# RWKV time mixing: both crossbar transposes in one-token rows, without shift copies

## The chip, the core and the metric

The kernel runs on one core of a Trainium2 chip. The metric is the time on the device in microseconds (us), median of several runs. A profile of one execution gives the span and what each engine did in it: TensorE (PE; PEld is its weight load), VectorE (DVE), ScalarE (ACT), GpSimd (POOL), and SyncE (SP), which here only issues DMAs.

## What is computed

The input x has 16 batches of 2048 tokens of 256 columns in float32. Each token is mixed with the one before it (the first token of a batch with zero), once for a value and once for a receptance; both go through a 256x256 matrix; the receptance goes through a sigmoid and gates the value; the product goes through a third matrix. The key is computed in the reference too, but nothing uses it.

```
x_prev[:, 1:] = x[:, :-1]
xv = x * time_mix_v + x_prev * (1 - time_mix_v)
xr = x * time_mix_r + x_prev * (1 - time_mix_r)
v = xv @ value_weight
r = xr @ receptance_weight
out = (sigmoid(r) * v) @ output_weight
```

## The kernel before

**Units.** A unit is 512 tokens of a batch, four units make a batch, and there are 64 of them. The matrices contract over the columns, so x must stand transposed in SBUF, with columns on the partitions (`xt`). For each unit g of the main loop (L614) TensorE makes the receptance (`psum_r`) and the value (`psum_v`) with `project`, four matmuls of 512 columns each, and the output (`psum_o`) of the unit before with eight matmuls of 256 columns (`out_matmuls`). ACT makes the sigmoid (`s_sb`, L626) and copies the output to SBUF (L440). VectorE multiplies the gate and the value (`z_sb`, L676).

**Mixing.** The coefficient of x is folded into the weights, so that the mixed operand is c * x_prev + x. The product c * x_prev (the "scaling") is made one or two units ahead, for a pair of units at once in the later part: half of it by VectorE (L340) or, from unit 34 (`FREE`) on, for one of the two operands by ACT (L606); the other half by GpSimd (L350). VectorE then adds x (L362). GpSimd's scaling of a unit is made to wait for a given addition of VectorE ("one at a time").

**Three ways into `xt`.** Batches 0 to 9 are loaded to SBUF as bf16 by GpSimd's DMAs (which cast) and transposed on TensorE (L274), with an ACT copy out of PSUM (L291). Batches 10 to 15 (`STAGED`) are cast into a DRAM buffer (`x_both` or `x_natural`) by the same kind of load, and go from there to SBUF by two DMA transposes on SP (`by_dma`, L247), one for 10 to 12 and one for 13 to 15. `T_AT` puts them at units 27 and 39.

- Batches 13 to 15: the DRAM buffer has one row per partition of x, 384 rows of 4096 columns (16 tokens each). In the transposed tile a token's predecessor stands in the slot before it, except for the first slot of each partition, which is filled by a shifted copy on ACT (`shift`, L639, two copies of 127 columns per batch, at the second unit of the batch before) and a memset on GpSimd (L220).
- Batches 10 to 12 (`NATURAL`): the DRAM buffer has one token a row, 256 columns, with 16 zero rows (`PAD`) ahead of each batch, written by six small DMAs on SP (L138): 6192 rows. In the transposed tile the predecessor is simply the column before, so `tokens` reads at an offset of one column and no shift is needed. The output of such a unit reads `z_sb` with a stride of four tokens (`natural=True`), and is stored in pieces of four rows of `out`.

**What keeps DMAs in order.** All stores but one are issued by SP, in program order; a pair of units is one store of 1 MB, named here by its odd unit (pair 25 is units 24 and 25). Each SP DMA waits for the eighth SP DMA before it, since eight semaphores are used in turn. [...] the first transpose waits for the whole of load 12, the loads of 13 to 15 (`STAGE_AT`, L685, issued by GpSimd at units 34, 35 and 36, behind its scaling in that unit) wait for the first transpose, and the second transpose waits for load 15. Loads 12 and 15 come as two halves (`HALVED`). `FIRST` names the pairs whose store is put off until just ahead of a transpose and waits for the first half of that load: pair 25 ahead of the first transpose, pair 29 ahead of the second. `WAITING` names the pairs whose store is put off until behind the second transpose: 31, 33 and 35. `dpool` has two DRAM buffers; output tiles come from `opool` (seven buffers) or, from pair 37 on, partly from `xpool`.

Of the kernel before, what the change touches and what calls it, by code (L numbers as in the profile page):

```python
# [9 lines left out]
BF16 = mybir.dt.bfloat16  # L10
# [5 lines left out]
def kernel(  # L16
# [37 lines left out]
    LONG = 8  # L54
    H = UJ // 2
    STAGED = 10
    BYDMA = NU - STAGED * UB
    CROSS = NU - BYDMA - LOOK
    FREE = CROSS
    LATE_O = CROSS - 2  # L60
    T_AT = {27: 10, 39: 13}
    FIRST = {25: 27, 29: 39}
    WAITING = {31: 39, 33: 39, 35: 39}
    STAGE_AT = {34: 13, 35: 14, 36: 15}
    GROUPS = [(2, 3), (4, 5, 6), (7, 8, 9), (10, 11, 12), (13, 14, 15)]
    HALVED = (12, 15)
    NATURAL = (10, 11, 12)
    PAD = 16
    SPARE = 9 * UB // 2
    NX, NO = 4, 7  # L70
# [19 lines left out]
    dpool = ctx.enter_context(tc.tile_pool(name="dpool", bufs=2, space=bass.MemoryType.DRAM))  # L90
    xtpool = ctx.enter_context(tc.tile_pool(name="xtpool", bufs=2))
# [15 lines left out]
    x_bf = {}  # L107
    x_both = {}
    loads = {}
    xt_both = {}  # L110
    xt = {}
# [17 lines left out]

    def new_staged(b, group):  # L130

        if b not in NATURAL:
            x_both[b] = dpool.tile([len(group), P, J, D], BF16, name="x_both")
            return
        x_both[b] = dpool.tile([len(group), PAD + S, D], BF16, name="x_natural")
        for h in range(KO):
            for k in range(len(group)):
                nc.sync.dma_start(  # L138
                    out=x_both[b][k, :PAD, h * P : (h + 1) * P], in_=zeros[k * PAD : (k + 1) * PAD]
                )  # L140

    def load(b):
        if b >= STAGED:
            group = next(q for q in GROUPS if b in q)
            if b == group[0]:
                new_staged(b, group)
            x_bf[b] = x_both[group[0]][b - group[0]]
            if b in NATURAL:
                x_bf[b] = x_bf[b][PAD:].rearrange("(p j) d -> p j d", p=P)
        else:  # L150
            x_bf[b] = xpool.tile([P, J, D], BF16, name="x_bf")
        if b < BYUNIT:
# [11 lines left out]
        return nc.gpsimd.dma_start(out=x_bf[b], in_=rows(b), max_dma_last_dim=run)  # L164
# [4 lines left out]
    for m, tm in enumerate([time_mix_r, time_mix_v]):  # L169
        nc.scalar.dma_start(  # L170
            out=tm_rows[m * KO : (m + 1) * KO, :], in_=tm.rearrange("(ko p) -> ko p", p=P)
        )

    def load_halves(e):
# [8 lines left out]
        out=w_f32[:, 0], in_=receptance_weight.rearrange("(ko p) n -> p ko n", p=P)  # L183
# [25 lines left out]
    def new_xt(b):  # L209
        if b >= BYUNIT:  # L210
            for group in GROUPS:
                if b != group[0]:
                    continue
                if b in NATURAL:
                    xt_both[b] = xtpool.tile([P, KO, len(group) * (PAD + S)], BF16, name="xt_both")
                    return
                xt_both[b] = xtpool.tile([P, J + 1, KO, len(group), P], BF16, name="xt_both")
                for k in range(len(group)):
                    xt[b + k] = xt_both[b][:, :, :, k]
                    nc.gpsimd.memset(xt[b + k][:, 0, :, 0:1], 0.0)  # L220
# [26 lines left out]
    def by_dma(b, after):  # L247

        new_xt(b)
        if b in NATURAL:  # L250
            op = nc.sync.dma_start_transpose(
                out=xt_both[b], in_=x_both[b].rearrange("b s d -> (b s) d")
            )
        else:
            op = nc.sync.dma_start_transpose(
                out=xt_both[b][:, 1:].rearrange("p j k b c -> p (j k) (b c)"),
                in_=x_both[b].rearrange("b p j d -> (b p) (j d)"),
            )
        tc.add_manual_dep(op.ins, after.ins.name, SYNC, reason="not beside a load")
        return op  # L260

# [54 lines left out]
    def slots(piece, off=0):  # L316

        b, _, lo, hi = piece
        j = lo // P + (lo // TU if b < BYUNIT else 0) + off
        return slice(j, j + (hi - lo) // P)  # L320

    def tokens(piece, off, ko=None):

        b, _, lo, hi = piece
        if b not in NATURAL:
            s = slots(piece, off)
            return xt[b][:, s] if ko is None else xt[b][:, s, ko]
        t = (b - NATURAL[0]) * (PAD + S) + PAD - 1 + off + lo
        cols = xt_both[NATURAL[0]][:, :, t : t + hi - lo].rearrange("p k (j c) -> p j k c", c=P)
        return cols if ko is None else cols[:, :, ko]  # L330

    def mixed(piece):
# [56 lines left out]
                stop=(n == len(parts) - 1),  # L389
            )  # L390

    def out_matmuls(ps, z, jj, slot, natural=False):
        by_slot = z.rearrange("p k (c j) -> p k j c" if natural else "p k (j c) -> p k j c", j=UJ)
        for ko in range(KO):
            nc.tensor.matmul(  # L395
                out=ps[:, slot, :],
                lhsT=by_slot[:, ko, jj],
                rhs=wo_bf[:, ko, :],
                start=(ko == 0),
                stop=(ko == KO - 1),  # L400
            )

    def store(queue, b, lo, hi, after=None):
        dst = out[b].rearrange("(p j) d -> p j d", p=P)
        src = o_sb[b, lo // (2 * UJ)]
        j = lo % (2 * UJ)
        op = queue.dma_start(out=dst[:, lo:hi, :], in_=src[:, j : j + hi - lo, :])
        if after is not None:
            tc.add_manual_dep(op.ins, after.ins.name, SYNC, reason="in turn with the last load")

    def out_part(pool, name, z, b, e, jj, n, copy, queue):
        ps = pool.tile([P, n, D], FP32, name=name)
        for k in range(n):
            out_matmuls(ps, z, jj + k, k)
# [12 lines left out]
    def output(g, z):  # L427
        b, e = divmod(g, UB)
        if e % 2 == 0:
            new_o(b, e // 2)  # L430
        o = o_sb[b, e // 2]
        j0 = e % 2 * UJ
        if g >= NU - 4:
            for h in range(2):
                out_part(ps_t_pool, "ps_t", z, b, e, h * H, H, nc.scalar.copy, nc.sync)
            return
        ps = ps_o_pool.tile([P, UJ, D], FP32, name="psum_o")
        for jj in range(UJ):
            out_matmuls(ps, z, jj, jj, b in NATURAL)
        nc.scalar.copy(out=o[:, j0 : j0 + UJ, :], in_=ps)  # L440
        if b < BYUNIT or b in NATURAL:
            if e % 2 == 1:
                nc.sync.dma_start(
                    out=unit_rows(out, b, e - 1, 2), in_=o.rearrange("p (e j) d -> p e j d", j=UJ)
                )
        elif g >= NU - 8:
            store(nc.sync, b, e * UJ, (e + 1) * UJ)
        elif e % 2 == 1:
            pair = (b, (e - 1) * UJ, (e + 1) * UJ)
            if g in FIRST:  # L450
                firsts.setdefault(FIRST[g], []).append(pair)
            elif g in WAITING:
                kept.setdefault(WAITING[g], []).append(pair)
            else:
                store(nc.sync, *pair)
# [158 lines left out]
    for g in range(NU - 1):  # L614
# [13 lines left out]
        if g in T_AT:  # L628
# [6 lines left out]
        by_crossbar = g // UB + 1 if g > CROSS and g % UB == 1 and g < NU - UB else None  # L635
        if by_crossbar in NATURAL:
            by_crossbar = None

        def shift(ko):  # L639
            if by_crossbar is not None:  # L640
                t = xt[by_crossbar]
                nc.scalar.copy(out=t[:, 0, ko, 1:P], in_=t[:, J, ko, 0 : P - 1])

        shift(1)
        if LATE_O < g < NU - 2:
            output(g - 2, z_prev2)
        shift(0)
        for p in products.get(g + 1, []):
            if g >= FREE and p[0][1] == 1:
                scale_act(p[0], (0,))  # L650
# [77 lines left out]
```

## Time and profile before

| what | us |
|---|---|
| median of 3 runs (lowest, highest) | 201.17 (200.4, 202.63) |
| the profiled execution | 201.63 |
| its span | 199.7 |
| PE busy | 191.9 |
| DVE busy | 185.0 |
| ACT busy | 178.2 |
| POOL busy | 83.9 |
| first transpose: issue, time to landing | 100.70, 17.7 |
| second transpose: issue, time to landing | 137.34, 17.3 |
| last matmul ends, last store issued | 194.3, 194.9 |

Times within a profile count from the start of the span. A line of the page's table of groups names the kernel's line, the engine, the operation and its operands; a timeline has start and duration in front, and in brackets how long the engine was idle before and whom it waited for. SPq is SP issuing DMAs; its duration is the issue, and the landing comes later. In the table by windows come, for PE, PEld, DVE, ACT and POOL, the busy time and the number of instructions, then the granted clock of TensorE, the mean share of the 16 DMA engines (over 1 when several packets are in flight in one engine) and the GB/s they moved.

### The profile page before, as it was taken

What the parts mean: (1) busy time and instruction counts of PE and PEld (TensorE: products, weight loads), DVE (VectorE), ACT (ScalarE), POOL (GpSimd) and SP (SyncE); (2) the same over time, 40 slices, a digit from 0 to 9 for tenths busy, and PEclk for the clock granted to TensorE, in tenths of its full rate; (3) what the DMA queues carried; (4) which work ended last, traced back from release to release, by engine and by line L of the source; (5) the groups of instructions that cost most, each with busy time, mean ns of one, the idle gap of its engine ahead of it and who ended that gap; (6) DMA issues with size and microseconds to landing.
All of it is one profiled execution on the core that took longest, in us unless ns stands there. A gap on an engine that the chain in (4) does not pass through costs nothing.

```text
span 199.7 us, 3815 instructions
## 1 busy us (share of the span) xinstructions
PE 191.9 (96%) x1389; PEld 123.7 (62%) x1389; DVE 185.0 (93%) x289; ACT 178.2 (89%) x203; POOL 83.9 (42%) x112
## 2 busy tenths in 40 slices
PE   8899999999999999999999998999999999999990
PEld 7456676666666666666666664666666665556660
DVE  1899999999999999999999999999999999999970
ACT  4699899999999999999999998999999999999970
POOL 1865543363542446332442437444444444444200
PEclk9999999999999999999999999999999999999998
DMA  5999999999999999999999999999999999999993
GB/s 174 229 189 216 216 281 273 277 283 274 291 313 292 217 265 279 322 288 315 334 406 251 207 359 200 215 197 275 209 241 346 440 405 403 408 404 431 396 382 133
DMA packets 37610, 58.10 MB, mean 291 GB/s; under 512 B 26068, under 2 KB 27352, under 8 KB 34520
## 3 DMA queue, kind: packets, MB, share of 16 engines
q1 hardware_dynamic: 33232, 41.34, 61.2%
q0 software_dynamic: 4208, 16.39, 41.5%
q8 instruction: 11, 0.18, 0.3%
q10 hardware_dynamic: 152, 0.13, 0.2%
q14 instruction: 7, 0.06, 0.1%
HBM read 34.34 MB, written 39.87 MB: 372 GB/s over the span
## 4 chain that ended last, share of the span: by engine, by line
PE 89%; DMA 4%; issue 1%; DVE 1%; ACT 1%; SPq 0%; POOL 0%; ACTq 0%
PE psum_v L370 27%; PE psum_r L370 26%; PE psum_o L395 26%; PE ps_t L274 8%; DMA x_bf<-in_x_dram 2%; DMA w_f<-n_receptance_weight_dram 2%; PE ps_t L395 1%; DVE z_sb L676 1%; ACT mix L606 1%; PE ps_t L370 0%; SPq L176 0%; POOL x_bf L194 0%; PE psum_r L395 0%; DVE x_bf L417 0%; PE psum_v L395 0%
## 5 line engine op out<-in xcount | busy, mean ns | idle before, releaser
L350 POOL TENSOR_SCALAR mix<-xt_both,c_sb 128x1024 bf16<-128x1024 bf16 (+1 forms) x55 | 61.2, 1113 | 87.7 <-DVE mix L362 87.7
L362 DVE TENSOR_TENSOR mix<-mix,xt_both 128x1024 bf16<-128x1024 bf16 x112 | 77.9, 705 | 1.4
L676 DVE TENSOR_TENSOR z_sb<-s_sb,psum_v 128x1024 bf16<-128x1024 bf16 (+1 forms) x64 | 76.7, 1200 | 2.4 <-PE psum_v L370 0.9
L370 PEld LDWEIGHTS <-w_bf 128*128 128x128 bf16 x516 | 48.9, 98 | 39.7 <-DVE mix L362 1.1
L626 ACT ACTIVATE s_sb<-psum_r 128x1024 bf16<-128x1024 f32 x63 | 65.2, 1036 | 6.0 <-PE psum_r L370 5.7
L370 PE MATMUL psum_v<-mix,w_bf 128*128 128x512 bf16 (+1 forms) x256 | 65.3, 377 | 0.3 <-DVE z_sb L676 0.2
L370 PE MATMUL psum_r<-mix,w_bf 128*128 128x512 bf16 (+1 forms) x252 | 64.2, 377 | 0.4 <-DVE mix L362 0.4
L395 PE MATMUL psum_o<-wo_bf,z_sb 128*128 128x256 bf16 x486 | 63.2, 273 | 0.0
L395 PEld LDWEIGHTS <-z_sb 128*128 128x128 bf16 x512 | 51.0, 101 | 18.7 <-DVE z_sb L479 0.8
L440 ACT COPY o_sb<-psum_o 128x1024 f32<-128x1024 f32 x50 | 51.2, 1024 | 4.9 <-PE psum_o L395 4.9
L291 ACT COPY xt_both<-ps_t 128x1024 bf16<-128x1024 bf16 x32 | 32.9, 1040 | 0.0
L274 PEld LDWEIGHTS <-x_bf 128*128 128x128 bf16 x304 | 19.6, 98 | 9.1 <-DMA x_bf<-in_x_dram 1.8
L274 PE MATMUL ps_t<-ident,x_bf 128*128 128x128 bf16 x304 | 22.7, 219 | 0.3 <-DMA x_bf<-in_x_dram 0.2
L340 DVE TENSOR_SCALAR mix<-xt_both,c_sb 128x1024 bf16<-128x1024 bf16 (+1 forms) x47 | 21.1, 458 | 0.0
L606 ACT ACTIVATE mix<-xt_both,c_sb 128x1024 bf16<-128x1024 bf16 x14 | 16.2, 1159 | 0.0
L362 DVE TENSOR_TENSOR mix<-mix,xt_first 128x1024 bf16<-128x1024 bf16 x15 | 10.6, 716 | 0.1
L440 ACT COPY x_bf<-psum_o 128x1024 f32<-128x1024 f32 x10 | 10.2, 1015 | 0.0
L340 DVE TENSOR_SCALAR mix<-xt_first,c_sb 128x512 bf16<-128x512 bf16 x22 | 6.5, 348 | 0.3 <-ACT xt_first L284 0.2
L291 ACT COPY xt_first<-ps_t 128x1024 bf16<-128x1024 bf16 x6 | 6.1, 1021 | 0.0
L164 POOL DMA_DIRECT2D x_bf<-in_x_dram x8 | 5.7, 714 | 0.0
L526 POOL COPY xt_first<-xt_first 128x254 bf16<-128x254 bf16 x5 | 2.0, 395 | 6.5 <-DVE mix L362 6.5
L350 POOL TENSOR_SCALAR mix<-xt_first,c_sb 128x512 bf16<-128x512 bf16 x6 | 4.1, 689 | 0.7 <-DVE mix L362 0.2
(72 smaller groups left out, 52.7 us busy)
## 6 DMA issues: line engine op xcount, KB each, us to landing
out_dram<-o_sb SPq DMA_DIRECT2D x24, 1024.0 KB, 15.9
x_bf<-in_x_dram POOLq DMA_DIRECT2D x8, 1024.0 KB, 19.1
out_dram<-x_bf SPq DMA_DIRECT2D x4, 1024.0 KB, 13.0
x_natural<-in_x_dram POOLq DMA_DIRECT2D x2, 1024.0 KB, 17.1
x_both<-in_x_dram POOLq DMA_DIRECT2D x2, 1024.0 KB, 9.4
x_bf<-in_x_dram POOLq DMA_DIRECT2D x6, 256.0 KB, 6.3
out_dram<-x_bf SPq DMA_DIRECT2D x6, 256.0 KB, 4.5
o_sb<-in_x_dram SPq DMA_DIRECT2D x4, 256.0 KB, 3.7
```

The costliest lines, as they stand in the source:

```text
L164: return nc.gpsimd.dma_start(out=x_bf[b], in_=rows(b), max_dma_last_dim=run)
L274: nc.tensor.transpose(out=ps[:, jj], in_=src[:, jj, ko * P : (ko + 1) * P], identity=idn)
L291: nc.scalar.copy(out=xt[b][:, j0 : j0 + UJ], in_=ps)
L340: nc.vector.tensor_scalar(out=mixed(piece)[:, :, ko], in0=tokens(piece, 0, ko), scalar1=c_sb[:, m, ko : ko + 1], scalar2=None, op0=ALU.mult,)
L350: op = nc.gpsimd.tensor_scalar(out=mixed(piece)[:, :, 1], in0=tokens(piece, 0, 1), scalar1=c_sb[:, m, 1:2], scalar2=1.0, op0=ALU.mult, op1 ...
L362: return nc.vector.tensor_tensor(out=mixed(piece), in0=mixed(piece), in1=tokens(piece, 1), op=ALU.add)
L370: nc.tensor.matmul(out=ps[:, mo, :], lhsT=w_bf[:, m, ko, mo * P : (mo + 1) * P], rhs=mixed((b, m, e * TU + lo, e * TU + hi))[:, :, ko], st ...
L395: nc.tensor.matmul(out=ps[:, slot, :], lhsT=by_slot[:, ko, jj], rhs=wo_bf[:, ko, :], start=(ko == 0), stop=(ko == KO - 1),)
L440: nc.scalar.copy(out=o[:, j0 : j0 + UJ, :], in_=ps)
L606: nc.scalar.activation(out=mixed(piece)[:, :, ko], in_=tokens(piece, 0, ko), func=ACT.Copy, scale=c_sb[:, m, ko : ko + 1],)
L626: nc.scalar.activation(out=s_sb, in_=ps_r, func=ACT.Sigmoid)
L676: nc.vector.tensor_tensor(out=z_sb[:, :, c : c + n], in0=s_sb[:, :, c : c + n], in1=ps_v[:, :, c : c + n], op=ALU.mult,)
```

## The change

Batches 13 to 15 are handled as 10 to 12 were. Both DRAM buffers have one token a row and are made at once, at the load of batch 10, so that twelve pad DMAs stand on SP where six stood. Both transposes have 6192 rows of 256 columns. `tokens` reads batches 10 to 15 at a column offset; the shift copies on ACT and the memsets for batches 13 to 15 go. The outputs of batches 13 to 15 are made with the stride over tokens and stored in pieces of four rows of `out` for a whole unit (of `n` rows for parts of a unit).

Three tables of the order change. The store of pair 23 is now the one just ahead of the first transpose, and that of pair 25 is put behind it. Pair 27 is the one just ahead of the second transpose, and pairs 29, 31, 33 and 35 stand behind it. Loads 13, 14 and 15 are issued at units 35, 36 and 37.

```diff
     T_AT = {27: 10, 39: 13}
-    FIRST = {25: 27, 29: 39}
-    WAITING = {31: 39, 33: 39, 35: 39}
-    STAGE_AT = {34: 13, 35: 14, 36: 15}
+    FIRST = {23: 27, 27: 39}
+    WAITING = {25: 27, 29: 39, 31: 39, 33: 39, 35: 39}
+    STAGE_AT = {35: 13, 36: 14, 37: 15}
-    NATURAL = (10, 11, 12)
...
     def new_staged(b, group):
-        if b not in NATURAL:
-            x_both[b] = dpool.tile([len(group), P, J, D], BF16, name="x_both")
-            return
         x_both[b] = dpool.tile([len(group), PAD + S, D], BF16, name="x_natural")
...
     def load(b):
         if b >= STAGED:
             group = next(q for q in GROUPS if b in q)
-            if b == group[0]:
-                new_staged(b, group)
-            x_bf[b] = x_both[group[0]][b - group[0]]
-            if b in NATURAL:
-                x_bf[b] = x_bf[b][PAD:].rearrange("(p j) d -> p j d", p=P)
+            if b == STAGED:
+                for q in GROUPS:
+                    if q[0] >= STAGED:
+                        new_staged(q[0], q)
+            x_bf[b] = x_both[group[0]][b - group[0], PAD:].rearrange("(p j) d -> p j d", p=P)
...
-                if b in NATURAL:
-                    xt_both[b] = xtpool.tile([P, KO, len(group) * (PAD + S)], BF16, name="xt_both")
+                if b >= STAGED:
+                    t = xtpool.tile([P, KO, len(group) * (PAD + S)], BF16, name="xt_both")
+                    for k in range(len(group)):
+                        xt[b + k] = t[:, :, k * (PAD + S) + PAD - 1 : (k + 1) * (PAD + S)]
+                    xt_both[b] = t
                     return
...
     def by_dma(b, after):
         new_xt(b)
-        if b in NATURAL:
-            op = nc.sync.dma_start_transpose(
-                out=xt_both[b], in_=x_both[b].rearrange("b s d -> (b s) d")
-            )
-        else:
-            op = nc.sync.dma_start_transpose(
-                out=xt_both[b][:, 1:].rearrange("p j k b c -> p (j k) (b c)"),
-                in_=x_both[b].rearrange("b p j d -> (b p) (j d)"),
-            )
+        op = nc.sync.dma_start_transpose(
+            out=xt_both[b], in_=x_both[b].rearrange("b s d -> (b s) d")
+        )
...
     def tokens(piece, off, ko=None):
         b, _, lo, hi = piece
-        if b not in NATURAL:
-            s = slots(piece, off)
-            return xt[b][:, s] if ko is None else xt[b][:, s, ko]
-        t = (b - NATURAL[0]) * (PAD + S) + PAD - 1 + off + lo
-        cols = xt_both[NATURAL[0]][:, :, t : t + hi - lo].rearrange("p k (j c) -> p j k c", c=P)
+        if b < STAGED:
+            cols = xt[b][:, slots(piece, off)]
+        else:
+            cols = xt[b][:, :, off + lo : off + hi].rearrange("p k (j c) -> p j k c", c=P)
         return cols if ko is None else cols[:, :, ko]
...
-    def out_matmuls(ps, z, jj, slot, natural=False):
-        by_slot = z.rearrange("p k (c j) -> p k j c" if natural else "p k (j c) -> p k j c", j=UJ)
-        for ko in range(KO):
+    def out_matmuls(ps, z, b, jj, n):
+        cols = z[:, :, jj * P : (jj + n) * P]
+        order = "p k (j c) -> p k j c" if b < STAGED else "p k (c j) -> p k j c"
+        slot = cols.rearrange(order, j=n)
+        for j in range(n):
+            for ko in range(KO):
...
     def store(queue, b, lo, hi, after=None):
-        dst = out[b].rearrange("(p j) d -> p j d", p=P)
         src = o_sb[b, lo // (2 * UJ)]
         j = lo % (2 * UJ)
-        op = queue.dma_start(out=dst[:, lo:hi, :], in_=src[:, j : j + hi - lo, :])
+        src = src[:, j : j + hi - lo, :]
+        if b < STAGED:
+            dst = out[b].rearrange("(p j) d -> p j d", p=P)[:, lo:hi, :]
+        else:
+            n = min(hi - lo, UJ)
+            dst = out[b, lo * P : hi * P].rearrange("(e p j) d -> p e j d", p=P, j=n)
+            src = src.rearrange("p (e j) d -> p e j d", j=n)
+        op = queue.dma_start(out=dst, in_=src)
...
-        def shift(ko):
-            if by_crossbar is not None:
-                t = xt[by_crossbar]
-                nc.scalar.copy(out=t[:, 0, ko, 1:P], in_=t[:, J, ko, 0 : P - 1])
-
-        shift(1)
         if LATE_O < g < NU - 2:
             output(g - 2, z_prev2)
-        shift(0)
```

More of the change, by code (lines that the diff above doesn't have):

```diff
@@ L390, in project_unmixed @@
             )
-    def out_matmuls(ps, z, jj, slot, natural=False):
-        by_slot = z.rearrange("p k (c j) -> p k j c" if natural else "p k (j c) -> p k j c", j=UJ)
-        for ko in range(KO):
[L395 to L401, printed above, removed]
+    def out_matmuls(ps, z, b, jj, n):
[4 more added lines that the diff above has]
+            for ko in range(KO):
+                nc.tensor.matmul(
+                    out=ps[:, j, :],
+                    lhsT=slot[:, ko, j],
+                    rhs=wo_bf[:, ko, :],
+                    start=(ko == 0),
+                    stop=(ko == KO - 1),
+                )
     def store(queue, b, lo, hi, after=None):
-        dst = out[b].rearrange("(p j) d -> p j d", p=P)
         src = o_sb[b, lo // (2 * UJ)]
         j = lo % (2 * UJ)
-        op = queue.dma_start(out=dst[:, lo:hi, :], in_=src[:, j : j + hi - lo, :])
+        src = src[:, j : j + hi - lo, :]
[6 more added lines that the diff above has]
+        op = queue.dma_start(out=dst, in_=src)
         if after is not None:
@@ L412, in out_part @@
         ps = pool.tile([P, n, D], FP32, name=name)
-        for k in range(n):
-            out_matmuls(ps, z, jj + k, k)
+        out_matmuls(ps, z, b, jj, n)
         lo = e * UJ + jj
@@ L437, in output @@
         ps = ps_o_pool.tile([P, UJ, D], FP32, name="psum_o")
-        for jj in range(UJ):
-            out_matmuls(ps, z, jj, jj, b in NATURAL)
+        out_matmuls(ps, z, b, 0, UJ)
         nc.scalar.copy(out=o[:, j0 : j0 + UJ, :], in_=ps)
-        if b < BYUNIT or b in NATURAL:
+        if b < BYUNIT:
             if e % 2 == 1:
@@ L634 @@
                 store(nc.sync, *pair)
-        by_crossbar = g // UB + 1 if g > CROSS and g % UB == 1 and g < NU - UB else None
-        if by_crossbar in NATURAL:
-            by_crossbar = None
-        def shift(ko):
-            if by_crossbar is not None:
-                t = xt[by_crossbar]
-                nc.scalar.copy(out=t[:, 0, ko, 1:P], in_=t[:, J, ko, 0 : P - 1])
-        shift(1)
         if LATE_O < g < NU - 2:
             output(g - 2, z_prev2)
-        shift(0)
         for p in products.get(g + 1, []):
```

## The prediction

> **What bounds the kernel now.** I read the page first, for the shares of the engines and of the DMA engines over time.
>
> ```profile
> PE 191.9 (96%) x1389; PEld 123.7 (62%) x1389; DVE 185.0 (93%) x289; ACT 178.2 (89%) x203; POOL 83.9 (42%) x112
> ...
> DMA  5999999999999999999999999999999999999993
> ...
> PE 89%; DMA 4%; issue 1%; DVE 1%; ACT 1%; SPq 0%; POOL 0%; ACTq 0%
> ```
>
> Two resources are full at once: TensorE (96% busy, 89% of the chain that ended last) and the DMA engines (9 tenths or more in every slice but the first and the last). A change that speeds up only one of them gains nothing where the other ends last. So the windows of the end come second.
>
> ```profile
> 150.00:155.00 5.00, 5.00 (x32) 3.22 (x31) 4.98 (x7) 4.59 (x6) 2.25 (x2) 1.00 1.18 361
> 155.00:160.00 5.00, 5.00 (x32) 3.22 (x31) 4.98 (x8) 4.99 (x8) 2.24 (x2) 1.00 1.00 419
> ...
> 170.00:175.00 5.00, 5.00 (x32) 2.94 (x31) 4.96 (x8) 4.55 (x5) 2.02 (x3) 1.00 1.02 406
> ...
> 190.00:195.00 5.00, 4.34 (x36) 3.00 (x34) 3.61 (x7) 3.74 (x8) 0.00 (x0) 1.00 1.00 377
> 195.00:200.00 5.00, 0.00 (x0) 0.00 (x0) 0.00 (x0) 0.00 (x0) 0.00 (x0) 0.80 0.33 115
> ```
>
> The last two columns are the DMA share and GB/s. From the end of the second transpose on, the DMA engines write output at about 400 GB/s without a pause until 195 us. The trace's landing records say the same: a store issued at 171.8 lands at 185.4, one issued at 187.45 lands at 192.5, the last one (128 KB), issued at 194.90, lands at 198.42. The queue of stores built up behind the transpose has only just run dry when the last unit is computed. By the trace's packet records the DMA engines carry 0.44 MB after 195.0, about 1.15 us of work at the 190 KB per 0.5 us that such small packets reach, and take until 198.
>
> Third, the SyncE queue in order of time, and who waits for whom.
>
> ```profile
> 60.66 35.23 SPq L407 DMA_DIRECT2D out_dram<-o_sb  x7
> 100.70 15.64 SPq L251 DMA_TRANSPOSE xt_both<-x_natural  x1
> 116.44 18.94 SPq L407 DMA_DIRECT2D out_dram<-o_sb  x2
> 137.34 13.82 SPq L255 DMA_TRANSPOSE xt_both<-x_both  x1
> 151.21 2.12 SPq L407 DMA_DIRECT2D out_dram<-o_sb  x3
> ...
> POOL x_both L164 <- DMA xt_both<-x_natural: 1.7, 1, 1.7
> ...
> PEld L370 <- DVE mix L362: 1.1, 2, 0.9
> ```
>
> The first transpose lands at 118.40, and the load of batch 13 (GpSimd, unit 34) waits 1.7 us for it. The timelines of three engines show what that costs:
>
> ```profile
> 118.93 0.57 POOL L164 DMA_DIRECT2D x_both<-in_x_dram  x1 [1.71 <-DMA xt_both<-x_natural]
> 119.53 1.13 POOL L350 TENSOR_SCALAR mix<-xt_both,c_sb 128x1024 bf16<-128x1024 bf16 x1
> ...
> 119.48 1.73 DVE L362 TENSOR_TENSOR mix<-mix,xt_both 128x1024 bf16<-128x1024 bf16 x1
> ...
> 121.27 1.04 PE L370 MATMUL psum_r<-mix,w_bf 128*128 128x512 bf16 x4 [0.44 <-DVE mix L362]
> ...
> 123.39 0.81 PE L370 MATMUL psum_v<-mix,w_bf 128*128 128x512 bf16 x3 [0.21 <-DVE z_sb L676]
> ...
> 155.09 0.30 ACT L642 COPY xt_both<-xt_both 128x127 bf16<-128x127 bf16 x1
> ```
>
> GpSimd's scaling behind the load starts about 1 us late, VectorE's addition takes 1.73 us where it otherwise takes 0.68, and TensorE loses 0.61 us before 121.27 (its group at 119.80 has 0.86 us of work) and 0.38 before 123.39: 1.0 us in all. It is the one stall of TensorE behind the start-up.
>
> **The skill.** "DMA: Bandwidth & Descriptors", section "Issuing engines are not separate DMA queues", says that all queues end on the same 16 DMA engines and only interleave; "Queues, rings and completion order" there says that each engine goes round the rings packet by packet, and takes one ring's descriptors in order. The trace agrees: between 72.5 and 75 us the loads' queue moves 352 KB and the stores' 353 KB, and the six pad writes of 4 KB each (L138) take 18.0 us to land behind a store and beside loads. So I count DMA work as one sum, and SyncE's DMAs as one line.
>
> **The change part by part.**
>
> *Both transposes in one-token rows.* It moves 6192 rows x 512 B = 3.17 MB against 3.15 MB: the same 256 B packets, 96 more of 12,384. At full rate both shapes move 565 packets in 0.5 us; with their pauses the first transpose (this shape) took 13.9 us from first to last packet, the second 14.2. I take -0.3; bounds -1 and +1, a pause.
>
> *Shift copies removed.* Six ACT copies of 0.32 us (L642). Pairs of units take 5.20 us where ACT has 0.41 us to spare; after each pair with a shift one of 5.24 follows. Worth 0 to 3 x 0.04 = 0.12 us of TensorE time. The shift for batch 13 was also the first reader of the second transpose (155.09, landed 154.68). Now GpSimd's scaling in unit 49 (nominally 155.9) and VectorE's at 157.54 are. GpSimd's three memsets for these batches go as well (0.18 us, hidden).
>
> *Operand layout.* Scalings read at an odd 2-byte offset and weights with a stride of four. Batches 10 to 12 already do so: L340 takes 478 ns in both, L350 1122 ns in both, and units take 2.60 us in both. Zero.
>
> *Stores of batches 13 to 15 in 4 KB pieces, not 8 KB.* In the trace 8 KB packets move 1049 KB in 2.5 us, 4 KB ones about 1005. Two pairs change: 2 x 2.5 us x 4% = +0.2 us of DMA.
>
> *Six more pad writes on SyncE near 52 us.* Each SyncE DMA waits for the eighth before it, so the stores of pairs 13 and 15 (their odd unit names a pair) are issued up to 11 us later than 60.66, and start moving near 78, not 71. Loads alone fill the engines meanwhile (100% share at 65 to 70 in this profile), and come earlier. Output buffers return after seven pairs: that of pair 13 is wanted at 96.6. Zero; up to +1 us if the loads run dry.
>
> *Store of pair 25 behind the first transpose.* All stores move by one place: 23 ahead of the first transpose and 25 behind it, 27 ahead of the second (with the first half of load 15), and 29, 31, 33, 35 behind it, where three stood. One 1 MB store fewer is ahead of the first transpose, which ends up to 2.5 us sooner. The price comes later: behind the second transpose stand 18 pairs (29 to 63) instead of 17. A store moves at 1.05 MB per 2.5 us: **+2.5 us** of DMA there.
>
> *Loads 13 to 15 one unit later.* Unit 35's scaling, no longer held up, starts near 118.5 (behind VectorE's additions that end at 118.36), takes 1.12, and load 13 is issued at 119.6, not 118.93: **+0.67 us**. The first transpose has landed by then: the 1.0 us stall goes. Loads 14 and 15 follow a unit later each, still ahead of the engines, since each load takes about 5 us against 2.6 us of a unit; GpSimd has 1.3 us free after a scaling, and two DMA issues take 1.09. Between store 25 (done by about 118.5) and the first packets of load 13 (1.5 us after issue, near 121) the DMA engines stand idle for 2 to 3 us, where there was no gap; that is the same loss seen from the front.
>
> **The sum.** Compute: -1.0 - 0.1 = 1.1 us sooner. DMA: second transpose ends +0.67 - 0.3 = 0.4 us later, at about 153.2, landing near 155.1; GpSimd's scaling, then due at 154.85, waits 0.3 us, which VectorE's addition at 158.6 doesn't see. Then +2.5 and +0.2: the queue is 3.1 us longer at the point that was 195.0. There the tail had slack: the 1.15 us of work left follows without gaps, to 195.0 + 3.1 + 1.15 = 199.25. With 0.65 us for uneven engines and landing, the last store lands at 199.9, not 198.42: **+1.5 us**. Compute's 1.1 us are not seen. The profiled execution took 201.63 (span 199.7), so 203.1 on its basis; the median of the runs shown is 201.17, so I give 202.7.
>
> **Rivals.**
>
> *The tail is latency, not a backlog, and compute sets the end (20%).* For it: the last store takes 3.5 us although the DMA share falls under 60% from 195.5 on. Then the stall's 1.0 and the shifts' 0.1 count: 201.17 - 1.1 = 200.1, faster than before. Against it: stores issued at 187 to 192 also take 4.5 to 5 us. It decides if the queue behind the second transpose is less than about 1.5 us longer than before.
>
> *The tail takes the whole 3.1 us (25%)*: if the last stores, each waiting for the eighth before it, still need their 3.5 us at the end of a longer queue, nothing is absorbed, and with a pause of the transpose it comes to +3.2: 204.4.
>
> *The second transpose comes too late for unit 52 (5%).* Landing after 156.5 would hold VectorE's scaling; it needs load 13 over 1.4 us later than I reckon. TensorE then stalls 1 to 2 us, mostly under the same DMA tail: 204.
>
> **The numbers.** Likeliest case, 50%: 202.7, own range 201.5 to 204. The range 200.0 to 204.8 leaves out the outer half of the first rival and the far end of the second. About 1% (2 us) is what a measurement of this kernel can tell from no change. Above 203.2 lie a third of the likeliest case and nearly all of the last two: 0.42. Below 199.2 lies a quarter of the first rival and little else: 0.07. The rest, 0.51, is within 1%.
>
> **What would show it.** Right: no wait of POOL's load for the first transpose and no wait of PE near 121; a DMA gap of 2 to 3 us near 119; second transpose issued near 138; four stores directly behind it; DMA share near 1.0 past 198 while PE ends near 193. Wrong: stores at 187 to 194 landing within 3 us, no gap near 119, or the second transpose issued before 137.

## The result, and the profile after

| what | before | after |
|---|---|---|
| median (lowest, highest), us, 6 runs each | 201.13 (200.4, 202.63) | 203.76 (203.13, 204.17) |
| ratio after to before, 95% interval | | 1.0123 [1.0085, 1.016] |
| the profiled execution, its span | 201.63, 199.7 | 203.89, 202.1 |
| last matmul ends | 194.3 | 194.5 |
| second transpose, first to last packet | 138.86 to 152.67 | 139.90 to 152.87 |
| DMA bytes that start to move after 195.0 | 573 KB | 1651 KB |
| last store issued, landed | 194.90, 198.42 | 198.13, 201.20 |

The change made the kernel 1.2% slower, clear of the noise. That is 1.06 us more than the 202.7 predicted, inside the range, and above 203.2, where the prediction had put a chance of 0.42. The page first, with the lines that stand against those of before:

```profile
PE 193.0 (95%) x1389; PEld 125.3 (62%) x1389; DVE 183.8 (91%) x289; ACT 177.1 (88%) x197; POOL 83.5 (41%) x109
...
DMA  5999999999999999999999959999999999999994
...
PE 80%; DMA 8%; DVE 5%; issue 1%; SPq 1%; POOL 1%; ACT 1%; DVEq 0%; ACTq 0%; POOLq 0%
```

In the row of 40 slices a 5 has appeared among the nines: slice 24, from 116 to 121 us. And the chain that ended last has twice the DMA share (8%, not 4%). The windows around the first transpose, in the kernel before:

```profile
100.00:105.00 5.00, 5.00 (x39) 3.29 (x38) 4.78 (x7) 4.60 (x6) 2.21 (x2) 1.00 1.13 394
115.00:120.00 5.00, 5.00 (x32) 3.03 (x31) 5.00 (x8) 4.55 (x5) 2.15 (x3) 1.00 1.17 353
120.00:125.00 5.00, 4.35 (x24) 2.16 (x23) 5.00 (x7) 4.03 (x5) 3.58 (x6) 1.00 1.01 203
```

And in the kernel after, there and at the end:

```profile
100.00:105.00 5.00, 5.00 (x43) 3.27 (x41) 4.78 (x10) 4.80 (x6) 1.23 (x2) 1.00 0.86 274
115.00:120.00 5.00, 5.00 (x32) 2.95 (x31) 5.00 (x8) 4.65 (x5) 2.06 (x3) 1.00 0.87 293
120.00:125.00 5.00, 5.00 (x33) 3.04 (x31) 5.00 (x8) 4.79 (x5) 3.07 (x5) 1.00 0.69 129
...
190.00:195.00 5.00, 4.38 (x35) 2.81 (x32) 3.47 (x7) 3.61 (x8) 0.00 (x0) 1.00 1.02 397
195.00:200.00 5.00, 0.00 (x0) 0.00 (x0) 0.00 (x0) 0.00 (x0) 0.00 (x0) 0.70 0.90 326
```

PE is busy for all of 120 to 125 (5.00, first number behind the length; before, 4.35), so the stall is gone. The DMA share (last column but one) falls from 1.17 and 1.01 to 0.87 and 0.69 where the gap was predicted, and from 1.13 to 0.86 near 103 where it was not. Behind 195 TensorE does nothing and the DMA engines work for most of five more us (0.90; before, 0.33). The SyncE queue:

```profile
52.34 20.05 SPq L134 DMA_DIRECT2D x_natural<-zeros  x12
73.34 23.50 SPq L409 DMA_DIRECT2D out_dram<-o_sb  x6
102.10 12.75 SPq L249 DMA_TRANSPOSE xt_both<-x_natural  x1
114.95 21.38 SPq L409 DMA_DIRECT2D out_dram<-o_sb  x2
138.55 12.79 SPq L249 DMA_TRANSPOSE xt_both<-x_natural  x1
151.39 3.47 SPq L409 DMA_DIRECT2D out_dram<-o_sb  x4
```

Twelve pads now hold the queue to 72.4; one store stands behind the first transpose and one ahead of the second (x2), and four behind that. GpSimd's timeline has load 13 without the wait for the transpose (before: 1.71 us in brackets):

```profile
119.49 1.12 POOL L342 TENSOR_SCALAR mix<-xt_both,c_sb 128x1024 bf16<-128x1024 bf16 x1 [1.31 <-DVE mix L354]
120.56 0.56 POOL L160 DMA_DIRECT2D x_natural<-in_x_dram  x1
```

That scaling waits for VectorE, as it does in every unit; the load stands behind it. 120.56 is not the 119.6 of the forecast, because all of this execution runs about 0.97 us later from its start: at 8.82 VectorE waited 0.8 us for the value weight's DMA (before: no wait, 7.76). The 1.0 us of stall that it no longer has gives that back, so the last matmul ends where it did (194.5). A late start is not what makes the end late: tables_only below starts 0.3 us behind before and loses as much.

### The profile page after: what moved, and what is told of

It reads as the page before. It is cut to its first block, busy times and chain, and to the rows that moved or that the text cites. A ratio compares the mean times of both kernels' runs of the same rounds, so it can differ in the third digit from the quotient of the medians.

```text
span 202.1 us, 3806 instructions
## 1 busy us (share of the span) xinstructions
PE 193.0 (95%) x1389; PEld 125.3 (62%) x1389; DVE 183.8 (91%) x289; ACT 177.1 (88%) x197; POOL 83.5 (41%) x109
## 4 chain that ended last, share of the span: by engine, by line
PE 80%; DMA 8%; DVE 5%; issue 1%; SPq 1%; POOL 1%; ACT 1%; DVEq 0%; ACTq 0%; POOLq 0%
PE psum_v L362 24%; PE psum_o L391 24%; PE psum_r L362 24%; PE ps_t L267 7%; DMA out_dram<-o_sb 5%; DMA w_f<-in_value_weight_dram 3%; DVE z_sb L665 2%; DVE mix L354 1%; DVE mix L332 1%; SPq L172 1%; ACT o_sb L440 1%; PE ps_t L362 0%; PE ps_t L391 0%; POOL x_bf L160 0%; POOL mix L342 0%
## 5 line engine op out<-in xcount | busy, mean ns | idle before, releaser
L354 DVE TENSOR_TENSOR mix<-mix,xt_both 128x1024 bf16<-128x1024 bf16 x112 | 76.6, 695 | 1.4
L391 PEld LDWEIGHTS <-z_sb 128*128 128x128 bf16 x512 | 51.7, 103 | 18.3 <-DVE z_sb L479 0.7
## 6 DMA issues: line engine op xcount, KB each, us to landing
out_dram<-x_bf SPq DMA_DIRECT2D x4, 1024.0 KB, 14.3
```

The lines of the kernel that those rows point to most:

```text
L354: return nc.vector.tensor_tensor(out=mixed(piece), in0=mixed(piece), in1=tokens(piece, 1), op=ALU.add)
L391: nc.tensor.matmul(out=ps[:, j, :], lhsT=slot[:, ko, j], rhs=wo_bf[:, ko, :], start=(ko == 0), stop=(ko == KO - 1),)
```

## The experiments

`REF` below stands for the tables of before (`FIRST = {25: 27, 29: 39}`, `WAITING = {31: 39, 33: 39, 35: 39}`, `STAGE_AT = {34: 13, 35: 14, 36: 15}`). Diffs are against the kernel after, that of tables_only against the kernel before. Ratios are to the kernel before on the same chip. The last five columns are of each kernel's profiled execution. "Idle" is what the DMA engines were short of full work between 60 and 194 us, added up from the packet records; durations of transposes are from first to last packet. "Last 573 KB" is the time from where 573 KB are left to the end of the last packet.

| kernel | ratio [95%] | median us | profiled us | idle us | transposes us | KB after 195.0 | last 573 KB took us |
|---|---|---|---|---|---|---|---|
| before | 1 | 201.13 | 201.63 | 0.6 | 13.9, 13.8 | 573 | 3.1 |
| after | 1.0123 [1.0085, 1.016] | 203.76 | 203.89 | 4.0 | 12.9, 13.0 | 1651 | 3.0 |
| layout_only | 0.9963 [0.9947, 0.9978] | 200.84 | 201.09 | 1.0 | 13.8, 12.4 | 656 | 2.7 |
| layout_store | 1.0015 [0.9992, 1.0037] | 201.94 | 203.57 | 1.1 | 15.3, 12.7 | 1463 | 2.7 |
| layout_loads | 0.9978 [0.9963, 0.9993] | 201.19 | 201.24 | 1.2 | 14.0, 13.1 | 723 | 2.7 |
| tables_only | 1.0142 [1.01, 1.0183] | 204.72 | 204.15 | 4.0 | 14.2, 13.0 | 1582 | 2.8 |
| fill_gap | 1.0027 [0.9997, 1.0058] | 202.07 | 201.34 | 1.0 | 13.6, 12.8 | 674 | 2.9 |
| merged_tail | 1.0163 [1.0126, 1.02] | 205.01 | 203.85 | 3.2 | 13.9, 12.9 | 1534 | 3.0 |
| two_behind | 1.023 [1.0188, 1.0272] | 206.42 | 205.73 | 5.5 | 13.8, 12.8 | 2364 | 3.0 |
| loads_two_later | 1.019 [1.0154, 1.0225] | 205.78 | 205.98 | 4.5 | 13.8, 14.8 | 2430 | 3.0 |
| layout_merged | 0.9986 [0.9966, 1.0006] | 201.40 | 201.40 | 1.0 | 13.8, 12.7 | 750 | 2.8 |
| layout_shifts | 0.9974 [0.9955, 0.9993] | 201.08 | 201.65 | 1.0 | 13.6, 12.8 | 863 | 2.2 |
| rows_of_before | 0.9963 [0.9942, 0.9984] | 200.72 | 200.37 | 1.7 | 13.8, 12.4 | 468 | 2.5 |
| tail_rows_of_before | 0.9965 [0.9946, 0.9985] | 200.96 | 200.96 | 0.8 | 14.3, 12.7 | 813 | 2.2 |

Three columns carry the study. The bytes that are left at 195.0 group the kernels as their profiled times do: 0.5 to 0.9 MB at 200.4 to 201.7 us, 1.5 to 1.7 MB at 203.6 to 204.2 and 2.4 MB at 205.7 to 206.0. That is close to bookkeeping, since what is left late must end late. The idle time says where it comes from: 0.6 to 1.7 us in the first group, 3.2 to 5.5 in the others. The one exception is layout_store (1.1 us, 1463 KB), whose first transpose was long. And the last 573 KB take 2.2 to 3.1 us, no less behind a long queue (2.7 to 3.0 in the six kernels with over 1 MB left) than behind a short one.

### Which part costs

**layout_only**: the new rows, with the order of before.

```diff
-    (the three tables of after)
+    REF
```

> The new layout with the three tables of before: both transposes in one-token rows, twelve pads, no shift copies, 4 KB store pieces; stores and loads in the order of before. If the order of stores and loads carries the loss (my theory), 17 pairs stand behind the second transpose as before, and the time is that of before plus 0.2 us for the smaller pieces: 201.3, ratio 1.000 to 1.003; the 1 us stall of TensorE near 121 comes back. If the layout itself carries it (pads holding up the stores, smaller pieces, the transpose), 203.5, ratio 1.012.

Measured 0.9963, under the 1.000 to 1.003 expected: a little faster than both kernels, the fastest full version of the study. The stall is back and the end is early:

```profile
120.00:125.00 5.00, 4.45 (x26) 2.25 (x24) 5.00 (x7) 4.32 (x5) 3.57 (x6) 1.00 1.01 184
...
195.00:200.00 5.00, 0.00 (x0) 0.00 (x0) 0.20 (x1) 0.00 (x0) 0.00 (x0) 0.74 0.38 131
```

TensorE loses 0.55 us in the first window, and it costs nothing that is seen: DMA share 1.01 there. So the layout is not the cause of the loss.

**layout_store**: the new rows and the moved stores, the loads at units 34 to 36.

```diff
-    STAGE_AT = {35: 13, 36: 14, 37: 15}
+    STAGE_AT = {34: 13, 35: 14, 36: 15}
```

> The new layout with the stores moved, but loads 13 to 15 at units 34 to 36 as before. My theory is that the loss is the time in which the DMA engines stand idle between the store behind the first transpose and load 13 (2.7 us in the changed kernel): here load 13 is issued near 117.8, without a wait for the transpose, the gap falls under 0.5 us, the second transpose is issued near 136, and the time is 201.2, ratio 1.000. If one more store behind the second transpose costs by itself, whatever happens ahead of it, 203.3 or more, ratio 1.011.

Measured 1.0015, and from 200.95 to 205.54, a wider spread than the others. The profiled execution is one of the long ones (203.57): its first transpose took 15.3 us, and load 13 waited for it:

```profile
119.39 0.57 POOL L160 DMA_DIRECT2D x_natural<-in_x_dram  x1 [1.38 <-DVE mix L354]
```

The line names VectorE; that it was the transpose is read from the times. The load comes 1.0 us behind the transpose's last packet here (118.39), in layout_only (118.13, load at 119.12) and in before (117.92, load at 118.93), where the profile does name the transpose. There is no gap near 119 (idle 0.2 us between 116 and 123, against 3.0 in after); slow packets within the transpose do not count as idle, and put 1463 KB behind 195.0 all the same. A load that stands ready behind the transpose starts when the transpose lands, so a transpose that ends sooner gives the moved megabyte back. That is how I read the median; it is not shown, since the only profile is of an execution in which it ended late. No run lets a load move beside a transpose, so what these waits cost by themselves stays open.

**layout_loads**: the new rows and the later loads, the stores where they were.

```diff
-    FIRST = {23: 27, 27: 39}
-    WAITING = {25: 27, 29: 39, 31: 39, 33: 39, 35: 39}
+    FIRST = {25: 27, 29: 39}
+    WAITING = {31: 39, 33: 39, 35: 39}
```

> The new layout with loads 13 to 15 one unit later, but the stores in the order of before (25 ahead of the first transpose, 17 pairs behind the second). My theory: the first transpose is as late as before, store 27 behind it ends near 120.5, load 13 follows near 121, a gap of 0.7 us or less; the stall goes; 201.9, ratio 1.004. If the later loads alone carry the loss, 203.3, ratio 1.011.

Measured 0.9978, where 1.004 was expected. The stall is gone without a price at the end:

```profile
115.00:120.00 5.00, 5.00 (x33) 2.96 (x31) 5.00 (x8) 4.55 (x6) 2.31 (x3) 1.00 1.20 358
120.00:125.00 5.00, 5.00 (x33) 2.95 (x31) 4.99 (x8) 4.59 (x6) 3.07 (x4) 1.00 0.87 172
...
195.00:200.00 5.00, 0.00 (x0) 0.00 (x0) 0.00 (x0) 0.00 (x0) 0.00 (x0) 0.62 0.41 145
```

**tables_only**: the kernel before, with the three tables of after.

```diff
-    FIRST = {25: 27, 29: 39}
-    WAITING = {31: 39, 33: 39, 35: 39}
-    STAGE_AT = {34: 13, 35: 14, 36: 15}
+    FIRST = {23: 27, 27: 39}
+    WAITING = {25: 27, 29: 39, 31: 39, 33: 39, 35: 39}
+    STAGE_AT = {35: 13, 36: 14, 37: 15}
```

> The kernel before with the three tables of the changed one: old layout for batches 13 to 15 with shift copies, stores moved and loads one unit later. My theory: the DMA gap near 119 is there, 18 pairs stand behind the second transpose, 203.5, ratio 1.011. If the layout carries the loss, 201.2, ratio 1.000.

Measured 1.0142, the whole loss without the new rows. Together: on the new rows, against layout_only, the store alone costs 0.5%, the loads alone 0.15% (the intervals touch), both 1.6%. The parts do not add. Each alone leaves the DMA engines no more idle than layout_only does (about 1 us), both together 4 us.

### Is the gap the cause?

**fill_gap**: everything as in after, but pair 27 also goes behind the first transpose, into the gap, and pair 29 takes its place ahead of the second, so that 17 pairs are left behind the second and not 18.

```diff
-    FIRST = {23: 27, 27: 39}
-    WAITING = {25: 27, 29: 39, 31: 39, 33: 39, 35: 39}
+    FIRST = {23: 27, 29: 39}
+    WAITING = {25: 27, 31: 39, 33: 39, 35: 39}
```

> The changed kernel with one more entry moved in the tables: store 27 is no longer put off until the second transpose but follows store 25 directly behind the first (29 is then the one just ahead of the second transpose, and 17 pairs stand behind it, not 18); loads stay one unit later. If the loss of the changed kernel is the DMA idle time of 2.7 us near 119, this fills it: gap under 0.5 us, last store landing near 198.5, 201.2, ratio 0.998 to 1.000, against 1.012 to 1.014 of the changed kernel and 0.998 of the variant that kept the old order of stores. If moving store 25 behind the first transpose costs by itself, ratio 1.008 or more.

Measured 1.0027, some 60% of the way back from after to layout_only: more than the 0.998 to 1.000 expected of the gap alone, and less than the 1.008 expected if the moved store costs by itself. In the profile the gap is closed and the tail is short:

```profile
100.00:105.00 5.00, 5.00 (x40) 3.29 (x38) 4.78 (x7) 4.59 (x6) 2.01 (x2) 1.00 0.93 269
115.00:120.00 5.00, 5.00 (x33) 3.04 (x32) 5.00 (x8) 4.55 (x6) 2.40 (x3) 1.00 1.13 412
120.00:125.00 5.00, 5.00 (x33) 2.96 (x31) 5.00 (x8) 4.59 (x6) 3.07 (x5) 1.00 1.03 221
...
195.00:200.00 5.00, 0.00 (x0) 0.00 (x0) 0.00 (x0) 0.00 (x0) 0.00 (x0) 0.62 0.37 135
```

412 GB/s where after had 293, 674 KB left at 195.0 and not 1651. The half per cent that is left against layout_loads I can place only in part: 0.5 us of idle time near 103 (share 0.93), where pair 23 is all that stands for the DMA engines once load 12 has ended. This execution (201.34) is also the shortest of its kernel, whose median is 202.07. The rest stays open.

**two_behind**: a step further the wrong way; two pairs (23 and 25 become 21 and 25 ahead, 19 pairs behind).

```diff
-    FIRST = {23: 27, 27: 39}
-    WAITING = {25: 27, 29: 39, 31: 39, 33: 39, 35: 39}
+    FIRST = {21: 27, 25: 39}
+    WAITING = {23: 27, 27: 39, 29: 39, 31: 39, 33: 39, 35: 39}
```

> The changed kernel with one more step of the same kind: the stores move by another place (21 ahead of the first transpose, 23 behind it, 25 ahead of the second, and 27, 29, 31, 33 and 35 behind it), so that 19 pairs stand behind the second transpose. If each pair that moves there leaves the DMA engines idle ahead of it for as long as its bytes take, the idle time up to 123 us grows from 3.9 to about 6.4 us and the time by 2.5 us: 206.2, ratio 1.024 to 1.027. If the first step's cost was a matter of that one store's place, ratio 1.013 to 1.016.

Measured 1.023, 1.1% more for one more megabyte, just under the 1.024 to 1.027 expected; the idle time grew to 5.5 us, not 6.4. The first transpose now starts at 99.0, lands sooner, and load 13 stands at 119.87 all the same:

```profile
115.00:120.00 5.00, 5.00 (x33) 2.97 (x31) 5.00 (x8) 4.55 (x6) 2.32 (x3) 1.00 0.31 131
120.00:125.00 5.00, 5.00 (x33) 2.96 (x31) 5.00 (x8) 4.59 (x6) 3.07 (x4) 1.00 0.83 154
...
195.00:200.00 5.00, 0.00 (x0) 0.00 (x0) 0.00 (x0) 0.00 (x0) 0.00 (x0) 0.81 1.02 380
200.00:205.00 5.00, 0.00 (x0) 0.00 (x0) 0.00 (x0) 0.00 (x0) 0.00 (x0) 0.50 0.26 93
```

PE is full from 115 to 125, the DMA engines are mostly empty at 115 to 120 (0.31; after, 0.87), and behind 195 they are full for five more us (1.02; after, 0.90).

**loads_two_later**: the stores in the order of before, the loads two units later than before.

```diff
-    (the three tables of after)
+    FIRST = {25: 27, 29: 39}
+    WAITING = {31: 39, 33: 39, 35: 39}
+    STAGE_AT = {36: 13, 37: 14, 38: 15}
```

> The new layout with the stores in the order of before and loads 13 to 15 at units 36, 37 and 38, two units later than before. 17 pairs stand behind the second transpose, but the DMA engines wait near 121 for load 13, which is issued near 122.3: idle about 3 us there, as in the changed kernel, but with no store moved. If idle DMA time is what costs, wherever it comes from, ratio 1.008 to 1.012 (1 unit later was 0.998, and 2.6 us are added, of which a part of the tail's slack is taken). If the loss needs the moved store, ratio 0.998 to 1.002.

Measured 1.019, more than any theory had said. The gap is made from the other side, with no store moved:

```profile
120.00:125.00 5.00, 5.00 (x33) 2.95 (x31) 5.00 (x8) 4.59 (x6) 2.57 (x4) 1.00 0.24 52
```

Load 13 is issued at 122.93. The idle time is a little longer than in after (4.5 us, not 4.0), and the second transpose is later and long (14.8 us):

```profile
141.25 14.63 SPq L249 DMA_TRANSPOSE xt_both<-x_natural  x1
```

It lands at 157.82, too late for unit 52, as the prediction's third rival had it. VectorE's scaling waits for it, GpSimd's starts at 158.00 after 3.84 us of idleness, and TensorE loses time twice:

```profile
157.85 0.49 DVE L332 TENSOR_SCALAR mix<-xt_both,c_sb 128x1024 bf16<-128x1024 bf16 x1 [0.70 <-DMA xt_both<-x_natural]
```

```profile
160.12 1.02 PE L362 MATMUL psum_v<-mix,w_bf 128*128 128x512 bf16 x4 [0.56 <-DVE z_sb L665]
...
161.53 1.04 PE L362 MATMUL psum_r<-mix,w_bf 128*128 128x512 bf16 x4 [0.39 <-DVE mix L354]
```

So DMA time left idle is paid at the end (2430 KB behind 195.0), whether a store was taken away or a load issued late. The transpose explains why it is more than expected: against layout_only it is issued 2.5 us later and its last packet comes 4.9 us later (157.37, 152.48), and the span is 4.9 us longer (204.2, 199.3). The five executions lie within 1 us (205.03 to 205.98), so this is hardly an accident of the profiled one. Part of it the packet records do explain: moved to a later time, this transpose has two loads of the kernel's own code beside it and not one, and stands still for 1.25 us at the second (last section).

### Is it the wait for the eighth store before?

**merged_tail**: after, with the stores of units 60 and 61 put together into 512 KB each, so that fewer stores stand in the last turns of the eight semaphores.

```diff
-    def store(queue, b, lo, hi, after=None):
+    def store(queue, b, lo, hi, after=None, n=UJ):
...
-            n = min(hi - lo, UJ)
+            n = min(hi - lo, n)
...
-                out_part(ps_t_pool, "ps_t", z, b, e, h * H, H, nc.scalar.copy, nc.sync)
+                out_part(ps_t_pool, "ps_t", z, b, e, h * H, H, nc.scalar.copy, None)
+            store(nc.sync, b, e * UJ, (e + 1) * UJ, n=H)
```

> The changed kernel with the stores of units 60 and 61 as one DMA of 512 KB each instead of two of 256 KB, so that the last store's eighth predecessor lies two stores further back. If the tail's slack is lost to that wait (last store issued at 198.1 though its data were ready near 195), the last store is issued 0.7 to 1 us earlier and the time falls by about as much: 203.3, ratio 1.008 to 1.010. If the tail is the backlog of bytes alone, no change: ratio 1.012 to 1.014.

Measured 1.0163, with an interval that overlaps that of after (five executions). The last store is issued at 197.24, not 198.13, and lands at 200.9, not 201.2: it is issued 0.9 us sooner and the landing moves by 0.3, as the whole queue does (573 KB are left at 197.54, not 197.85). The median did not fall. **layout_merged**, the same edit on layout_only:

> The new layout with the tables of before, and the stores of units 60 and 61 merged as in the run before. There the last store was issued at 195.3, about 0.3 us behind its data, so the wait for the eighth predecessor hardly binds: ratio 0.995 to 0.997, no more than 0.2 us better than without the merge (0.9963). If the size of the DMAs themselves counts, 0.5 us better; if the later start of the first half's store counts, up to 0.5 us worse.

Measured 0.9986, against 0.9963 without it: no gain there either. So nothing shows the wait for the eighth store to set the end.

### Where does the layout's 0.4% come from?

**layout_shifts**: layout_only with six copies of 127 columns on ACT, into a scratch tile, where the shift copies stood.

```diff
+                nc.scalar.copy(out=scratch[:, ko, 1:P], in_=xt[shifted_b][:, ko, 1:P])
```

> The new layout with the tables of before, plus six ACT copies of 127 columns at the places of the removed shift copies; they read batches 13 to 15 and write a scratch tile that nothing reads. If the 0.7 us gain of the layout is the shift copies, the time goes back to that of before: ratio 0.999 to 1.000. If it is the transposes or the stores, it stays at 0.996 to 0.997; by the trace of before the copies are worth 0.1 us at most.

Measured 0.9974 [0.9955, 0.9993], between the two: most of the gain stays without them, but the interval reaches into the 0.999 to 1.000 expected of the copies, so whether they make a part of it these runs do not tell.

**rows_of_before**: layout_only, with batches 13 to 15 stored into the rows of before (8 KB pieces; their output rows are in another order).

```diff
-        if b < STAGED:
+        if b < STAGED or b >= STAGED + 3:
```

> The new layout with the tables of before, and the stores of batches 13 to 15 into the rows of out that the kernel before used (pieces of 8 KB for a pair, parts of a unit at a pitch of 16 KB); so their rows of out stand in another order within the batch. If the layout's gain of 0.4% over before comes from the stores (the last ones landed 3.1 us after issue, in the kernel before 3.5), ratio 0.999 to 1.001. If it comes from the transpose or the ACT copies, ratio 0.996 to 0.997.

**tail_rows_of_before**: the same for the last four units only.

```diff
-        if b < STAGED:
+        if b < STAGED or b * UB + lo // UJ >= NU - 4:
```

> As the run before, but only the stores of the last four units go into the rows of the kernel before (at a pitch of 16 KB); rows of batch 15 stand in another order. If the gain of the layout is the sooner landing of the last stores, ratio 0.999 to 1.000; if it is in the larger stores or elsewhere, 0.996 to 0.997.

Measured 0.9963 and 0.9965, as layout_only: the size of the stores' pieces is worth nothing that these runs can tell, neither on the whole nor at the end. Of what is left, the traces differ in the second transpose: 13.8 us in before, 12.4 to 13.1 in the new shape where no other thing was late. But tables_only has the old shape and took 13.0, and the transpose of before has a standstill of 0.9 us near 141.3 that tables_only lacks. The pads and the memsets were not tried alone. So the source of the 0.4% stays open.

## Why the prediction was right, and where a term was off

- *Both resources full, and the DMA queue behind the second transpose sets the end*: right. The 1.0 us stall of TensorE is gone in layout_loads, whose last matmul ends at 193.85 and not at 194.74 as in layout_only, which has the stall; both spans are 199.3 us (ratios 0.9978 and 0.9963). So the first rival (compute sets the end, 200.1) falls.
- *Load 13 issued at 119.6; a gap of 2 to 3 us near 119*: right. The gap adds up to 3.0 us between 116 and 123. In five profiles with loads at unit 35 (tables_only, layout_loads, fill_gap, merged_tail, two_behind) the issue is at 119.8 to 119.9. Not foreseen: another 0.86 us near 103, where pair 23 alone is too little to keep the engines busy to the first transpose's first packet. Against these 3.4 us of new idle time stands a first transpose that took 0.9 us less than that of before.
- *Second transpose ends 0.4 us later, at 153.2*: 152.87, with the start of the whole execution late by 0.97. The page "DMA: Bandwidth & Descriptors", section "Latency and other measured facts", of the Trainium skill gives a DMA transpose 261 GB/s where the middle dimension is not contiguous, and about 350 to 400 in the contiguous case. Here 3.17 MB in 12.4 to 15.3 us are 207 to 256 GB/s for rows without gaps: under the lower figure even at best, and the same shape differs by 2.9 us from one execution to the next. A shape's gain of 0.3 us could not have been read from one profile of each. Its source was a misreading besides: the prediction has 14.2 us for the second transpose of before, and its packets run from 138.86 to 152.67, 13.8 us, no longer than the first. That the end came out near the forecast is luck: the late start and a transpose 0.8 us shorter than that of before (13.0, 13.8) cancel.
- *A queue 3.1 us longer at the point that was 195.0*: the point at which 573 KB are left moves from 195.0 to 197.86, **+2.9**. Right.
- *Tail slack: 1.15 us of work, and 0.65 for uneven engines and landing, so that of 3.1 us only 1.5 are seen*: **this is the term that was mis-sized.** Measured by its packets, the tail of before took 3.1 us for 573 KB, not 1.8. 131 KB of it stood on ACT's queue and were not counted (0.44 MB is SP's queue alone), and its packets, mostly of 1 KB, moved 492 KB in 1.5 us, 164 in half a microsecond and not 190. The other 81 KB took as long again, while the DMA share fell to 0.28, 0.18 and 0.07. The drain is as long behind a longer queue (3.0 us), so it absorbed nothing: the last store lands 2.8 us later. Of these the span shows 2.4, since it ends 0.9 us behind the last landing and not 1.3.
- *The rival that the tail takes the whole 3.1 us (204.4)* was right that nothing is absorbed, but its reason is not borne out: an earlier issue of the last store changed nothing (merged_tail). The result lies between this rival and the likeliest case.
- *Rows, shift copies, 4 KB pieces, pads*: costed at nothing or at 0.3 us. Together with the order of before they are worth -0.4%, some 0.8 us. The pads, which hold SyncE's queue to 72.4 us, cost no DMA time: the DMA engines are never idle between 60 and 95 us.
- *What was not put together*: the forecast had the moved store and the late load as two terms (+2.5 and +0.67) and noted that the gap is "the same loss seen from the front". The runs say how they belong together: the moved megabyte is lost where load 13 stands at a fixed place, while with the load waiting behind the transpose (layout_store) two thirds of the loss are gone from the median.

## What to carry to other kernels

Where the DMA engines are full to the end, add up the time in which they are not, from the packet records, wherever it lies: here it came back at the end about one for one (layout_only to two_behind: 4.5 us more idle time, 4.7 us more span). In bytes left at 195.0 that is 2.75 us per megabyte (656 KB and 199.3 us, 2364 KB and 204.0 us). It does not count slow packets in a transpose, which put bytes off to the end as well (layout_store). A transfer that a wait releases and one that stands at a fixed place in an engine's program behave differently when the work ahead of them is moved; removing a wait from a program can open a gap that the wait had closed. Do not count a draining tail as slack unless a trace shows that it gets shorter when work is put ahead of it.

## What the runs showed of the hardware

- A DMA transpose of 6192 rows of 512 B moves 565 packets of 256 B in 0.5 us (289 GB/s) where it runs freely. At that rate its 12,384 packets would take 11.0 us; the 26 of this shape in the 14 traces took 12.4 to 15.3 us from first to last packet.
- Each of the 28 transposes, of either shape, stands still while a packet moves of the kind that the page calls "instruction", which by its name is the program's own code. It has queues of its own (before):

```profile
q8 instruction: 11, 0.18, 0.3%
q14 instruction: 7, 0.06, 0.1%
```

Each first transpose has one 16 KB packet of q8 beside it (at 110.92 us in before) and each second one an 8 KB packet of q14 (148.32). From 0.2 to 0.6 us behind the start of such a packet, nearly no packet of the transpose starts, for 1.45 to 1.5 us in the first transpose and for 0.8 to 0.9 in the second. The standstill goes with the code and not with a place in the transpose: it begins 11.4 us into the first transpose of two_behind and 7.4 us into that of layout_only, 0.5 us behind the packet in both. The second transpose of loads_two_later has both kinds beside it (148.24 and 153.82) and stands still twice, for 0.9 and 1.25 us. Beside plain stores a 16 KB code packet (175.83 in before) leaves no mark: 1008 KB in those 2.5 us, 1004 and 1028 in those around them. The DMA share hides it, because packets under way count as busy (1.3 all along); the bytes moved show it. Why a transpose stops is not shown.
- Besides this, transposes run slowly in their first microseconds, to a different extent each time, the first of layout_store stood still three more times for 0.35 to 0.4 us, and the second of before once for 0.9 us (141.3), with no code packet near. The cause of these stays open.
- The last 573 KB, in packets of 1 and 2 KB on SP's and ACT's queues, take 2.2 to 3.1 us in the 14 kernels. In the first 1.5 us they move at 140 to 185 KB in 0.5 us; in the rest, of 0.7 to 1.6 us, 35 to 65 KB move in the first half microsecond and then under 30. With packets of 4 KB the stores move 201 KB in 0.5 us, with 8 KB 210.
